# x's wide rows in four strided groups at the head of the program, y's wide rows on ScalarE's queue beside them

## The chip, the cores and the metric

The kernel runs on one core of one Trainium2 chip. The metric is device time in microseconds (us); the kernel before takes 119.74 us, the median of three runs (119.72 to 119.80). A core has engines that compute (VectorE and ScalarE here, DVE and ACT in the profile) and 16 DMA engines that move data between HBM, the chip's main memory, and SBUF, the on-chip memory of 128 partitions. SyncE (SP) computes nothing here: it issues DMAs. A DMA that is issued from SP shows in the profile as queue q1, one issued from ScalarE as q10.

## The reference

Two float32 arrays of 1024 x 4096 (16.8 MB each) are multiplied element by element, and the tanh form of GELU is applied to the product:

```
z = x * y
return (0.5 * z * (1 + np.tanh(np.sqrt(2 / np.pi) * (z + 0.044715 * z ** 3)))).astype(np.float32)
```

So 33.55 MB must be read from HBM and 16.78 MB written. Nothing is reduced or reused.

## The kernel before

The work is element by element, so the arrays are taken as flat memory. `columns` (L51) cuts each into three consecutive pieces, and each piece into 128 contiguous rows, one per partition: piece 0 has rows of 1280 elements (5 KB), piece 1 rows of 16384 (64 KB), piece 2 rows of 15104 (60,416 bytes). x stays whole in SBUF (`xs`), and the result is written over it. y has a smaller buffer (`ys`, 20,440 elements a partition): the later pieces of y go where earlier ones have been used up, so the loads of y wait for products.

The scheduling framework is closed before the first instruction (L58, L59): everything after it is in the order written, with hand-made semaphores. The order of y is piece 1, piece 2, piece 0.

- `_hoist` (L25) takes a DMA out of its place and puts it into the program's first block, ahead of the barrier with which a program opens.
- Loads before the change: x piece 0 (5 KB rows) is hoisted on SP (L79); x piece 1 (64 KB rows) is hoisted on ScalarE's queue (L80). SP then waits until x piece 0 has landed (L81), issues y piece 1 (L82) and x piece 2 (L83). It waits for the third product, issues y piece 2, waits for the fourth product, issues y piece 0 (L84 to L87).
- Compute (L91 to L109): VectorE waits for the pieces of x and y, multiplies in steps of 4096 columns (four, piece 1), 2048 and 768 (eight, piece 2) and 1280 (one, piece 0), at L98. After each product ScalarE applies GELU in place (L106).
- Stores (L111 to L115), all from SP: piece 1 once y piece 2 has landed and its GELUs are done, then piece 2, then piece 0, each when its last GELU is done. SP waits for the stores and clears the semaphores (L116 to L121).

A DMA adds 16 to its semaphore when it has landed, one for each DMA engine that carried part of it.

Of the kernel before, what the change touches and what calls it, by code (L numbers as in the profile page):

```python
# [1 line left out]

# [4 lines left out]


F32 = mybir.dt.float32
GELU = mybir.ActivationFunctionType.Gelu_apprx_tanh  # L10

PIECES = [(0, 1280), (1280, 17664), (17664, 32768)]

Y_LOADS = [(1280, 17664, 4056), (17664, 32768, 0), (0, 1280, 15104)]

Y_FREE = [0, 3, 4]

STEPS = [[4096] * 4, [2048] * 7 + [768], [1280]]  # L20
STORES = [(1280, 17664), (17664, 32768), (0, 1280)]
Y_BUF = 20440


def _hoist(nc, issued):  # L25

    here = nc.cur_bb.bb.instructions
    first = nc.main_func.blocks[0].instructions
    for ins in issued:
        del here[next(k for k, i in enumerate(here) if i is ins or i.name == ins.name)]  # L30
    engine = issued[0].engine
    at = next(
        k
        for k, i in enumerate(first)
        if i.engine == engine and type(i).__name__ == "InstDrain"
    )
    first[at:at] = issued


@with_exitstack  # L40
def kernel(
    ctx: ExitStack,
    tc: tile.TileContext,
    x: bass.AP,
    y: bass.AP,
    out: bass.AP,
):
    nc = tc.nc
    P = nc.NUM_PARTITIONS

    def columns(t, a, b):  # L51

        flat = t.flatten_outer_dims().rearrange("r c -> (r c)")
        pa, pb = next(q for q in PIECES if q[0] <= a and b <= q[1])
        return flat[P * pa : P * pb].rearrange("(p c) -> p c", p=P)[:, a - pa : b - pa]


    tc.close()  # L58
    tc.compile()  # L59

    xs = nc.alloc_sbuf_tensor("xs", [P, PIECES[-1][1]], F32).ap()
    ys = nc.alloc_sbuf_tensor("ys", [P, Y_BUF], F32).ap()
    sem_x = [nc.alloc_semaphore(f"sem_x{i}") for i in range(len(PIECES))]
    sem_y = [nc.alloc_semaphore(f"sem_y{i}") for i in range(len(Y_LOADS))]
    sem_mul = nc.alloc_semaphore("sem_mul")
    sem_act = nc.alloc_semaphore("sem_act")
    sem_o = [nc.alloc_semaphore(f"sem_o{i}") for i in range(len(STORES))]

    def load_x(i, engine=nc.sync):
        a, b = PIECES[i]  # L70
        return engine.dma_start(out=xs[:, a:b], in_=columns(x, a, b)).then_inc(sem_x[i], 16)

    def load_y(i):
        a, b, r = Y_LOADS[i]
        return nc.sync.dma_start(
            out=ys[:, r : r + b - a], in_=columns(y, a, b)
        ).then_inc(sem_y[i], 16)

    _hoist(nc, [load_x(0).ins])  # L79
    _hoist(nc, [load_x(1, nc.scalar).ins])  # L80
    nc.sync.wait_ge(sem_x[0], 16)  # L81
    load_y(0)  # L82
    load_x(2)  # L83
    for i in range(1, len(Y_LOADS)):  # L84
        if Y_FREE[i]:
            nc.sync.wait_ge(sem_mul, Y_FREE[i])
        load_y(i)  # L87

    n = 0
    done = {}  # L90
    for i, (a, b, r) in enumerate(Y_LOADS):  # L91
        for j, (xa, xb) in enumerate(PIECES):
            if xa <= a < xb:
                nc.vector.wait_ge(sem_x[j], 16)
        nc.vector.wait_ge(sem_y[i], 16)  # L95
        c = a
        for w in STEPS[i]:
            nc.vector.tensor_mul(  # L98
                out=xs[:, c : c + w],
                in0=xs[:, c : c + w],  # L100
                in1=ys[:, r + c - a : r + c - a + w],
            ).then_inc(sem_mul, 1)
            n += 1
            done[c + w] = n
            nc.scalar.wait_ge(sem_mul, n)
            nc.scalar.activation(  # L106
                out=xs[:, c : c + w], in_=xs[:, c : c + w], func=GELU
            ).then_inc(sem_act, 1)
            c += w  # L109

    for i, (a, b) in enumerate(STORES):  # L111
        if i == 0:
            nc.sync.wait_ge(sem_y[-2], 16)
        nc.sync.wait_ge(sem_act, done[b])
        nc.sync.dma_start(out=columns(out, a, b), in_=xs[:, a:b]).then_inc(sem_o[i], 16)  # L115
    for i in range(len(STORES) - 1):  # L116
        nc.sync.wait_ge(sem_o[i], 16)
    nums = sorted(s.num for s in [*sem_x, *sem_y, *sem_o[:-1], sem_mul, sem_act])
    assert nums == list(range(nums[0], nums[-1] + 1))
    nc.sync.sem_clear(range(nums[0], nums[-1] + 1))  # L120
    nc.sync.wait_ge(sem_o[-1], 16).then_inc(sem_o[-1], -16)  # L121


# [1 line left out]
_INS = ['x', 'y']  # L125
_OUTS = [((1024, 4096), 'float32')]


# [23 lines left out]
```

## Time and profile before

| what | value |
|---|---|
| median of three runs | 119.74 us |
| span of the profiled execution, first to last instruction | 118.5 us |
| execution's time beyond the span | about 1.2 us (119.74 less 118.5) |
| HBM read and written | 33.55 MB and 16.78 MB, 425 GB/s over the span |
| VectorE busy | 35.2 us (30%) |
| ScalarE busy | 31.0 us (26%) |
| x piece 0, issue to landing | 13.6 us |
| x piece 1, issue to landing | 30.4 us |
| y piece 1, issue to landing | 29.0 us |
| x piece 2, issue to landing | 46.5 us |
| y piece 2, y piece 0, issue to landing | 22.5 us, 19.7 us |
| three stores, issue to landing | 20.4, 20.9, 20.8 us |

How to read it: times in the trace start at the span's first instruction. "DMA share" is the busy share of the 16 DMA engines. In a narrow window a transfer row is counted by its start and with its whole length, so a share can be over 100% there; in wide windows this evens out. From the share of a queue, the width of the window and the number of packets the mean time of one row follows: share x 16 x width / packets. A packet is one row of one partition, or the 4-byte completion write that each DMA engine makes after its rows. There are 8 rows and one completion write of each DMA on each DMA engine (9 DMAs x 16 x 9 = 1296 packets).

### The profile page before, as it was taken

To read this page: it belongs to the slowest core of one execution; us is meant where nothing else is said; L and a number is where in the kernel's file an instruction comes from. 1 tells how busy PE (TensorE), PEld (TensorE's weight loads), DVE (VectorE), ACT (ScalarE), POOL (GpSimd) and SP (SyncE) were. 2 spreads that over 40 slices of the span, in tenths; PEclk is the share of its full clock that TensorE was granted. 3 is DMA by queue.
4 is the path that set the end of the run, shared out by engine and by line. 5 is a ranking of instruction groups with operands and counts; after the bars stand their busy time and mean duration, and the time that the engine had idled before them with its cause. 6 is when DMAs were issued, how large, how long until landed. Compare 5 with 4: busy or idle time off the path is not lost.

```text
span 118.5 us, 82 instructions
## 1 busy us (share of the span) xinstructions
DVE 35.2 (30%) x13; ACT 31.0 (26%) x14; POOL 0.2 (0%) x4
## 2 busy tenths in 40 slices
DVE  0000000000000069999920000059999940000000
ACT  4000000000000000977975000006998990000000
POOL 0000000000000000000000000000000000000000
DMA  9888899889988897797797797798899887977975
GB/s 492 382 382 382 354 575 487 354 354 398 664 354 354 354 652 326 326 652 326 326 632 347 326 632 347 326 575 354 354 531 531 354 354 326 652 326 326 652 326 221
DMA packets 1296, 50.33 MB, mean 425 GB/s; under 512 B 144, under 2 KB 144, under 8 KB 528
## 3 DMA queue, kind: packets, MB, share of 16 engines
q1 hardware_dynamic: 1152, 41.94, 82.2%
q10 hardware_dynamic: 144, 8.39, 16.5%
HBM read 33.55 MB, written 16.78 MB: 425 GB/s over the span
## 4 chain that ended last, share of the span: by engine, by line
DMA 55%; DVE 24%; ACT 3%; issue 1%; DVEq 0%
DMA ys<-in_y_dram 43%; DVE xs L98 24%; DMA xs<-in_x_dram 11%; ACT xs L106 3%; DVEq L95 0%
## 5 line engine op out<-in xcount | busy, mean ns | idle before, releaser
L98 DVE TENSOR_TENSOR xs<-xs,ys 128x2048 f32<-128x2048 f32 (+3 forms) x13 | 35.2, 2777 | 60.9 <-DMA ys<-in_y_dram 60.9
L106 ACT ACTIVATE xs<-xs 128x2048 f32<-128x2048 f32 (+3 forms) x13 | 29.7, 2301 | 65.1 <-DVE xs L98 65.1
L106 ACT ACT_TABLE_LOAD x1 | 1.3, 1283 | 1.6 <-PEq L59 1.6
L136 POOL MEMSET const-bfloat16-1.0<- 128x1 bf16 x1 | 0.1, 103 | 0.0
L136 POOL MEMSET const-uint8-127<- 128x1 uint8 x1 | 0.1, 102 | 0.0
L136 POOL MEMSET const-float32-0.0<- 128x1 f32 x1 | 0.1, 100 | 0.2 <-issue 0.2
L136 POOL MEMSET const-float32-1.0<- 128x1 f32 x1 | 0.1, 99 | 0.0
## 6 DMA issues: line engine op xcount, KB each, us to landing
xs<-in_x_dram SPq DMA_DIRECT2D x1, 7552.0 KB, 46.5
ys<-in_y_dram SPq DMA_DIRECT2D x1, 7552.0 KB, 22.5
out_dram<-xs SPq DMA_DIRECT2D x1, 7552.0 KB, 20.4
xs<-in_x_dram SPq DMA_DIRECT2D x1, 640.0 KB, 13.6
ys<-in_y_dram SPq DMA_DIRECT2D x1, 640.0 KB, 19.7
out_dram<-xs SPq DMA_DIRECT2D x1, 640.0 KB, 20.8
xs<-in_x_dram ACTq DMA_DIRECT2D x1, 30.4
ys<-in_y_dram SPq DMA_DIRECT2D x1, 29.0
```

The costliest lines, as they stand in the source:

```text
L98: nc.vector.tensor_mul(out=xs[:, c : c + w], in0=xs[:, c : c + w], in1=ys[:, r + c - a : r + c - a + w],).then_inc(sem_mul, 1)
L106: nc.scalar.activation(out=xs[:, c : c + w], in_=xs[:, c : c + w], func=GELU).then_inc(sem_act, 1)
L136: nc = _bacc.Bacc("TRN2", target_bir_lowering=False, num_devices=1)
```

## The change

x piece 1 is cut into four DMAs, each of every fourth partition (0, 4, 8, ..., then 1, 5, 9, ...), 32 rows of 64 KB each, all adding to one semaphore. The first is hoisted on SP and is the first instruction of the program. y piece 1 is hoisted on ScalarE's queue, where x piece 1 was. SP issues the other three groups, x piece 0 and x piece 2 right after the opening barrier, without waiting for anything to land. VectorE waits for 64 counts on x piece 1 instead of 16. The loads of y pieces 2 and 0, the compute and the stores stay as they were.

```diff
+GROUPS = 4
...
-    def load_x(i, engine=nc.sync):
+    def load_x(i, group=slice(None)):
         a, b = PIECES[i]
-        return engine.dma_start(out=xs[:, a:b], in_=columns(x, a, b)).then_inc(sem_x[i], 16)
+        return nc.sync.dma_start(
+            out=xs[group, a:b], in_=columns(x, a, b)[group]
+        ).then_inc(sem_x[i], 16)
 
-    def load_y(i):
+    def load_y(i, engine=nc.sync):
         a, b, r = Y_LOADS[i]
-        return nc.sync.dma_start(
+        return engine.dma_start(
             out=ys[:, r : r + b - a], in_=columns(y, a, b)
         ).then_inc(sem_y[i], 16)
 
-    _hoist(nc, [load_x(0).ins])
-    _hoist(nc, [load_x(1, nc.scalar).ins])
-    nc.sync.wait_ge(sem_x[0], 16)
-    load_y(0)
+    groups = [slice(g, None, GROUPS) for g in range(GROUPS)]
+    _hoist(nc, [load_x(1, groups[0]).ins])
+    _hoist(nc, [load_y(0, nc.scalar).ins])
+    for group in groups[1:]:
+        load_x(1, group)
+    load_x(0)
     load_x(2)
     for i in range(1, len(Y_LOADS)):
-        if Y_FREE[i]:
-            nc.sync.wait_ge(sem_mul, Y_FREE[i])
+        nc.sync.wait_ge(sem_mul, Y_FREE[i])
         load_y(i)
...
-                nc.vector.wait_ge(sem_x[j], 16)
+                nc.vector.wait_ge(sem_x[j], 16 * GROUPS if j == 1 else 16)
```

## The prediction

> **What bounds the kernel now.** I read the page first: slices, queues, chain. Then I asked the trace for stretches of time, to see where the 16 DMA engines are not moving bytes at full pace, and for the DMA queues in narrow windows, to get the time of one row.
>
> From the page:
>
> ```profile
> DVE 35.2 (30%) x13; ACT 31.0 (26%) x14; POOL 0.2 (0%) x4
> ...
> DMA packets 1296, 50.33 MB, mean 425 GB/s; under 512 B 144, under 2 KB 144, under 8 KB 528
> ...
> q1 hardware_dynamic: 1152, 41.94, 82.2%
> q10 hardware_dynamic: 144, 8.39, 16.5%
> ...
> DMA 55%; DVE 24%; ACT 3%; issue 1%; DVEq 0%
> ```
>
> The two queues together use 98.7% of the 16 engines' span, so the bound is DMA throughput. The chain names VectorE for 24% of the span, and that is misleading: while it multiplies, the queue still holds transfers. The stretches show it (length, DVE, ACT, POOL, clock, DMA share, GB/s):
>
> ```profile
> 0.00:1.00 1.00, 0.00 (x0) 0.00 (x0) 0.20 (x4) 1.00 0.00 0
> 1.00:2.30 1.30, 0.00 (x0) 0.73 (x1) 0.00 (x0) 1.00 0.93 295
> 2.30:78.20 75.90, 17.43 (x4) 15.02 (x5) 0.00 (x0) 1.00 1.00 433
> 78.20:79.10 0.90, 0.75 (x1) 0.00 (x0) 0.00 (x0) 1.00 0.90 376
> 79.10:118.10 39.00, 17.02 (x9) 15.26 (x9) 0.00 (x0) 1.00 1.00 430
> 118.10:118.50 0.40, 0.00 (x0) 0.00 (x0) 0.00 (x0) 1.00 0.00 0
> ```
>
> From 2.3 us to 118.1 us the engines are busy all the time but for a dip at 78.2 to 79.1. What a reordering of loads can win lies in three places: the first 1.0 us, in which nothing moves; the opening up to about 5 us; the dip. The chain in order of time tells which waits order the queue:
>
> ```profile
> 0.00 13.55 DMA xs<-in_x_dram
> ...
> 13.57 28.99 DMA ys<-in_y_dram
> ...
> 42.66 13.11 DVE xs L98 x3
> ...
> 55.78 22.47 DMA ys<-in_y_dram
> ```
>
> **The price of a row.** Queue lines of five narrow windows, in this order: 0 to 2.3 us (opening, 5 KB rows), 2.3 to 2.65 (first 64 KB rows), 5.0 to 5.4 (second 64 KB rows), 7.6 to 8.2 (third), 62 to 77 (60,416-byte rows):
>
> ```profile
> q1 hardware_dynamic: 75, 0.38, 52.6%
> ...
> q10 hardware_dynamic: 16, 1.05, 726.8%
> ...
> q10 hardware_dynamic: 16, 1.05, 609.8%
> ...
> q10 hardware_dynamic: 16, 1.05, 403.2%
> ...
> q1 hardware_dynamic: 102, 6.16, 94.8%
> ```
>
> Share x 16 x width / packets gives the mean row. Opening 5 KB rows: 0.526 x 16 x 2.3 / 75 = 258 ns; in 77.6 to 79.0, in full flow, the same rows take 197 ns. 64 KB rows: 2544 ns the first, 2439 the second, 2419 the third. 60,416-byte rows: 2231 ns. So each DMA engine must work 24 x 2.42 + 24 x 2.231 + 24 x 0.197 = 116.35 us, whatever the order. The span is 118.52: 1.0 before the first packet, 0.4 from the last packet to the end, and 0.75 to be found. The opening has 0.09 of idle time (0.07 of 1.3 us), 75/16 x (258 - 197) = 0.29 of slow 5 KB rows, and 0.12 + 0.02 of slow first and second 64 KB rows: 0.52. The dip is 0.09.
>
> **The spread of the 16 engines.** In the trace's record of single packets the engines take their first row between 1.01 and 1.49 us. The completion counts of x piece 0 come in from 13.01 to 13.55, those of y piece 1 from 42.01 to 42.56, those of y piece 2 from 77.71 to 78.25. So a spread of 0.54 arises in the opening and is carried unchanged. It costs at the dip: SP issues the first store only when the slowest engine has counted (78.27), its first rows start at 79.11, and the faster engines are out of work before.
>
> **The change, part by part.**
>
> *Bytes and row lengths* are the same: 0.
>
> *Completion writes.* Three more DMAs put three more 4-byte writes on each engine, 9 ns each in the packet records: +0.03 us.
>
> *Issuing.* One DMA issue takes SP 0.33 to 0.43 us. Five stand behind the barrier now (three groups, x pieces 0 and 2); the trace has SP through it at about 1.5 us, so they run to about 3.5 us. Cover: group 0 gives each engine two rows of 2.42 us, from 1.0 to 5.8 us even without y, and group 1, issued by 1.9, should flow at 3.0. SP's wait for x piece 0 (12.0 us) goes, and nothing is queued behind it that is late: 0. If the group DMAs took long to issue, the 2.8 us of margin would be used up first.
>
> *x and y piece 1 side by side.* Each engine alternates between the queues: 16 rows x 2.42 = 38.7 us, so both land at about 40.5 instead of 30.4 and 42.6. VectorE starts 2 us earlier, which is worth nothing by itself: y piece 2 is issued after the third product, 40.5 + 13.1 = 53.6, while x pieces 0 and 2 keep the queue busy until 40.2 + 8 x 0.197 + 8 x 2.231 = 59.6. Cover 6.0 us, less 0.9 from issue to flow. Alternation itself costs nothing where it is seen: from 17 to 29 us, with x and y rows of 64 KB alternating, the packet records show 2.42 us a row and no idle time. The new case differs in that both run at the same row number, so I allow 0 to 0.1.
>
> *The second half* keeps its order. y piece 2 still ends the loads but for y piece 0; VectorE needs 15.5 us from there, ScalarE the rest, and the second store is issued at 96.55 while the first one still flows until 98.7. Margin 2.1 us, unchanged: 0.
>
> *The opening*, the one term that counts. x piece 0's rows leave it and are paid at 197 ns in the middle: -0.29 at most. In their place come 64 KB rows of x, then of y. Lower bound of what these cost at a cold start: as the second rows, 0.02 for each tensor, and no idle time: 0.04, a gain of 0.48. Upper bound: the chill of 0.29 belongs to the first half microsecond of traffic whatever its shape, and x's first and y's first rows each pay 0.12 on top, with 0.09 idle and 0.02 as now: 0.64, a loss of 0.12. I take what the nearest row shows, the first 64 KB rows: 0.12 for x, 0.12 for y, 0.09 idle, 0.02 = 0.35, a gain of 0.17.
>
> *The spread.* The first DMA has 32 rows instead of 128, so the last engine should get its first row sooner. Bounds: the spread stays (0), or vanishes, and the slowest engine moves from its 78.25 to the mean of 77.97 (-0.28). I take half: -0.13.
>
> Sum: -0.17 - 0.13 + 0.03 = -0.27 us. The profiled span of 118.52 becomes 118.25, and with the same 1.2 us beside it 119.47. The bounds added up: -0.73 at one end, +0.25 at the other.
>
> [...] The row: one 128-row DMA of x piece 1 flows at 2.42 us a row on every engine, and no 32-row DMA is in this trace. [...]
>
> **The rivals.**
>
> *The opening costs the same whatever row opens it* (-0.05 to +0.25 us: 119.69 to 119.99). For it: the first 5 KB packets end between 1.44 and 1.77 us however early they start, so something warms up by the clock, not by rows. Against: ten of the sixteen first 64 KB rows pay again, at 2.3 us.
>
> *A group does not spread evenly* (slower). Every forecast above needs each group to put two rows on every engine, at full pace. If a group's 32 rows run on half of the engines, or on all but two at a time into one lane of SBUF, then x piece 1's 8 rows for an engine count double: 8 x 2.42 = +19.3 us, about 139 us. It decides as soon as one engine has three rows of a group instead of two (+2.4 us). Nothing of it shows in a trace with 128-row DMAs only; against it speaks that 4 x 32 rows stepped by four touch each run of four partitions once, as the 128-row DMA does four times. [...]
>
> *The change is hidden anyway.* If the spread and the chill stay as they are, 0.03 us of completion writes is all: 119.77.
>
> **How the numbers follow.** A cheaper opening as summed, 119.2 to 119.65: 0.56, of which 0.45 lies below 119.50. Same opening or hidden, 119.65 to 119.98: 0.23. Opening dearer by more than 0.24 us: 0.06. Uneven groups: 0.15. A measurement of this kernel can hardly tell less than 0.2%, 0.24 us, from no change. So faster 0.45; same 0.11 + 0.23 = 0.34; slower 0.06 + 0.15 = 0.21. The likeliest case's own range is 119.2 to 119.65. The range given leaves out the uneven groups and the thin ends: 119.1 to 120.0.
>
> **What would show it.** Right: first rows of 64 KB near 2.54 us, first starts closer together than 0.48 us, completion counts of y piece 2 within 0.3 us, the last of them before 78.1, x and y piece 1 landing at 40 to 41 us, a DMA share of 1.00 from 2 us on. Wrong: 64 KB rows over 2.45 us on q1 after 5 us (lanes shared), engines that idle before 40 us (uneven groups), idle engines about 3 to 8 us (late groups), a spread of 0.5 us as before. Wrong for another reason: a first packet that starts later than 1.0 us, which no row here prices.

## The result, and the profile after

The changed kernel takes 120.25 us (median of four runs, 120.16 to 120.37) against 119.73 us for the kernel before on the same chip: ratio 1.0041, 95% interval 1.0028 to 1.0054. It is slower by about half a microsecond, where the forecast was 119.47 us. The profiled execution has a span of 118.84 us and took 120.18 us.

The page of the changed kernel, with the lines that answer those of before (the bound is still DMA throughput; 48 more packets are the three additional DMAs with one completion write on each of 16 engines):

```profile
DVE 35.2 (30%) x13; ACT 31.0 (26%) x14; POOL 0.2 (0%) x4
...
DMA packets 1344, 50.33 MB, mean 424 GB/s; under 512 B 192, under 2 KB 192, under 8 KB 576
...
q1 hardware_dynamic: 1200, 41.94, 81.8%
q10 hardware_dynamic: 144, 8.39, 16.9%
...
DMA 53%; DVE 23%; ACT 3%; SPq 1%; issue 1%; DVEq 0%
```

Stretches of the changed kernel (length, DVE, ACT, POOL, clock, DMA share, GB/s):

```profile
0.00:1.00 1.00, 0.00 (x0) 0.00 (x0) 0.20 (x4) 1.00 0.00 0
1.00:4.10 3.10, 0.00 (x0) 1.28 (x1) 0.00 (x0) 1.00 1.01 338
4.10:78.50 74.40, 17.43 (x4) 14.47 (x4) 0.00 (x0) 1.00 1.00 432
78.50:79.50 1.00, 0.82 (x1) 0.00 (x0) 0.00 (x0) 1.00 1.47 615
79.50:118.40 38.90, 16.96 (x9) 15.26 (x9) 0.00 (x0) 1.00 0.98 425
118.40:118.80 0.40, 0.00 (x0) 0.00 (x0) 0.00 (x0) 1.00 0.01 0
```

From 4.1 us on nothing is worse than before: 432 GB/s up to 78.5 us, where it was 433, and from 78.5 to 118.4 us 429 GB/s, as in the 39.9 us from 78.2 to 118.1 before (a row counts where it starts, so the 615 and the 425 of the two lines belong together). In 1.0 to 4.1 us the engines count as busy (a share of 1.01), yet only 338 GB/s pass, where a share of 1.00 goes with 432 GB/s afterwards: here busy was not the same as moving at full pace. The queue lines of three narrow windows, 1.1 to 1.9 us (first rows of y piece 1), 4.1 to 4.7 (first rows of x piece 1) and 6.6 to 7.2 (second rows of y), tell what is slow:

```profile
q10 hardware_dynamic: 16, 1.05, 391.9%
...
q1 hardware_dynamic: 16, 1.05, 407.4%
...
q10 hardware_dynamic: 16, 1.05, 403.2%
```

Share x 16 x width / 16 packets: 3135 ns, 2444 ns, 2419 ns. The rows that opened the traffic lost 0.72 us on each engine. The first of them came from ScalarE's queue: SP's strided issue took 0.54 us instead of 0.38, and x's first rows found the engines already taken by y.

The chain in order of time shows that everything downstream kept its distance:

```profile
2.99 38.33 DMA xs<-in_x_dram
...
41.34 13.11 DVE xs L103 x3
...
54.47 24.12 DMA ys<-in_y_dram
```

VectorE starts 1.3 us earlier and y piece 2 is asked for 1.3 us earlier, but it lands at 78.59 instead of 78.25: the queue is full anyway (a share of 1.00 up to 78.5 us), and what was lost at the opening is still missing at the end. Bytes moved tell the same: summed over the packet records, the changed kernel is 0.15 MB behind the kernel before at 10 us, which is 0.34 us at full pace, and it is still 0.34 us behind at 110 us.

**A single number for an opening.** From the packet records I take the mean end of each engine's first wide row (64 KB), subtract that row at full pace (2.42 us) and the narrow rows done before it at their full pace (0.197 us for a 5 KB row, shorter rows in proportion). What is left is the moment from which full pace would have given the same progress; I call it the effective start, counted from the first DMA issue. Before: 5.00 - 2.42 - 0.98 = 1.60 us. After: 4.43 - 2.42 = 2.01 us. The difference, 0.41, and the completion writes, 0.03, are more than the span's growth in these two profiles (0.32, from 118.52 to 118.84); a second profile of the changed kernel had 118.98, and by its packet records 0.1 us of that was lost at the dip near 79 us.

### The profile page after: what moved, and what is told of

Same layout as the page of the kernel before. It is cut to its first block, busy times and chain, and to the rows that moved or that the text cites. A ratio compares the mean times of both kernels' runs of the same rounds, so it can differ in the third digit from the quotient of the medians.

```text
span 118.8 us, 85 instructions
## 1 busy us (share of the span) xinstructions
DVE 35.2 (30%) x13; ACT 31.0 (26%) x14; POOL 0.2 (0%) x4
## 4 chain that ended last, share of the span: by engine, by line
DMA 53%; DVE 23%; ACT 3%; SPq 1%; issue 1%; DVEq 0%
DMA xs<-in_x_dram 32%; DVE xs L103 23%; DMA ys<-in_y_dram 20%; ACT xs L111 3%; SPq L73 1%; DVEq L100 0%
## 5 line engine op out<-in xcount | busy, mean ns | idle before, releaser
L103 DVE TENSOR_TENSOR xs<-xs,ys 128x2048 f32<-128x2048 f32 (+3 forms) x13 | 35.2, 2779 | 61.3 <-DMA xs<-in_x_dram 41.3
```

Of the source, the lines that this page charges most:

```text
L103: nc.vector.tensor_mul(out=xs[:, c : c + w], in0=xs[:, c : c + w], in1=ys[:, r + c - a : r + c - a + w],).then_inc(sem_mul, 1)
```

## The experiments

**Theory A**: wide rows are slow to get going when nothing else is in flight, and x piece 0's narrow rows covered that. **Theory B**: the strided groups cost, by their longer issues. Later rivals: two queues that open together (C); a cold start that belongs to the addresses a row touches (A2) and not to time or to the first rows of any kind (A1); a fixed moment of the clock; collisions of rows a power of two apart. The batches ran on different chips, each beside the kernel before on its own chip, whose median was 119.70 to 119.91 us; ratios are to those.

### One group instead of four

```diff
-GROUPS = 4
+GROUPS = 1
```

> x piece 1 as one 128-row load at the head of SP, the rest as in the changed kernel (y piece 1 opens ScalarE's queue, x piece 0 later). Theory A (wide rows open cold: the first 64 KB rows of a program take about 3.1 us instead of 2.42, as the changed kernel's profile shows, whatever their grouping): no better than the changed kernel, 120.1 to 120.4 us, first rows of y again 2.9 to 3.4 us. Theory B (the strided groups cost: SP needs 0.47 to 0.59 us for each instead of 0.38, and x's rows come late): back to about 119.7 us, first rows near 2.5 us.

Measured: 120.13 us, 1.0018 (1.0008 to 1.0027); first rows of x, now 16 from SP, in the window 1.0 to 2.0 us:

```profile
q1 hardware_dynamic: 16, 1.05, 320.2%
```

3202 ns. The slow first rows are there without groups and on the other queue. The time left room for B, so the changed kernel was run again, first on another chip:

> The changed kernel once more, beside the next three on one chip. Theory A alone (wide rows open cold, the grouping is free): the same ratio as with one group, 1.0018, and the span of 118.8 us again. Theory A and B together: 1.003 to 1.005, so 0.2 us or more above the kernel with one group.

Measured: 120.36 us, 1.0056 (1.0042 to 1.0069). Across chips this seemed to speak for B. Then both stood on one chip:

> The changed kernel, beside the kernel with one group on the same chip. If wide rows that open idle DMA engines are the whole cause, both have the same ratio to before, within 0.1%. If the four strided issues cost too, this one is 0.1 to 0.4% above the other.

> x piece 1 in one group, beside the changed kernel on the same chip. Wide opening the whole cause: the same ratio as the changed kernel, 1.002 to 1.005. Grouping costs as well: 0.1 to 0.4% below it.

Measured: four groups 120.30 us, 1.0037 (1.0024 to 1.0050); one group 120.19 us, 1.0032 (1.0020 to 1.0044). The grouping costs 0.1 us by the medians, and the two intervals overlap; together they would still leave room for about 0.3 us. Most of the loss, by the medians, is there without it. The gap between the first two batches, 1.0018 and 1.0056, does not return on one chip.

### x piece 0 back in the opening

The changed kernel with x piece 0 at the head and all four groups behind the barrier:

```diff
-    _hoist(nc, [load_x(1, groups[0]).ins])
+    _hoist(nc, [load_x(0).ins])
     _hoist(nc, [load_y(0, nc.scalar).ins])
-    for group in groups[1:]:
+    for group in groups:
         load_x(1, group)
-    load_x(0)
```

> x piece 0 (5 KB rows) opens SP again, y piece 1 opens ScalarE's queue, x piece 1 in its four strided groups behind the barrier. Theory A: the 5 KB rows take the cold start, the first rows of y take about 2.55 us as x's did before, 119.7 to 119.8 us. Theory B: four strided groups are still issued, 120.1 to 120.3 us.

Measured: 119.91 us, 1.0001 (0.9992 to 1.0010), where the kernel before took 119.91 us on this chip. The whole loss is gone, with the strided groups, y on ScalarE's queue and the missing wait all kept. First rows of y, window 2.0 to 2.42 us:

```profile
q10 hardware_dynamic: 16, 1.05, 624.3%
```

2622 ns. At 10 us this run is 0.04 us behind the kernel before by bytes moved, where the changed kernel is 0.34. (Its profiled execution was the slowest of its twelve, 120.48 us; it lost its time later, between 45 and 80 us.) A holds, B falls.

The kernel before without its wait (`nc.sync.wait_ge(sem_x[0], 16)` taken out):

> The kernel before without SP's wait for x piece 0, so y piece 1 follows right behind the barrier and x and y piece 1 alternate from the start. Theory A: the opening is the same 5 KB rows, so 119.7 us as before (within 0.1). Rival (side-by-side streams of x and y from the start cost): 119.9 us or more. Theory B says nothing here but 119.7.

Measured: 119.94 us, 0.9998 (0.9989 to 1.0006). The 119.9 us named for the rival is reached in absolute time only because this chip ran the kernel before in 119.91 us; the ratio decides. The wait was worth nothing; streams of x and y side by side from the start cost nothing that shows within 0.1%.

### How much cover is needed

One group of x piece 1 behind the barrier, y piece 1 on ScalarE's queue ahead of it, and as the opening all, half or a quarter of x piece 0's columns (the rest later):

```diff
-    _hoist(nc, [load_x(1, groups[0]).ins])
+    _hoist(nc, [load_x(0, 0, 640).ins])      # 320, 640 or all 1280 columns
     _hoist(nc, [load_y(0, nc.scalar).ins])
...
+    load_x(1)
+    load_x(0, 640)
```

> All of x piece 0 (5 KB rows) opens SP, y piece 1 ScalarE's queue, x piece 1 whole behind the barrier. Full cover: 0.999 to 1.0005 of before, wide first rows near 2.55 us, although y opens instead of x and x and y alternate.

> Half of x piece 0 (640 columns, 2.5 KB rows) opens SP, y piece 1 ScalarE's queue, x piece 1 whole behind the barrier. If narrow rows only cover the 0.8 us that wide rows need longer to get going, half the cover (8 rows of about 0.1 us, flowing until about 2.1 us) gives back about half: 0.1 to 0.25 us over the run with all 1280 columns.

> A quarter of x piece 0 (320 columns, 1,280-byte rows, eight for each engine) opens SP, y piece 1 opens ScalarE's queue, x piece 1 whole behind the barrier. If the cold start passes with time or with the first rows of any kind (A1), y's first 64 KB rows take at most 2.7 us and the time is 0.999 to 1.0005 of before. If it belongs to the addresses that a row touches (A2), they take 3.0 us or more, as they are y's first, and the time is 1.0015 to 1.003.

Measured, with the run without cover for comparison; effective start by the packet records:

| narrow rows in the opening | ratio to before (95%) | effective start, us |
|---|---|---|
| 1280 columns, 5 KB | 1.0006 (0.9997 to 1.0014) | 1.64 |
| 640 columns, 2.5 KB | 1.0015 (1.0006 to 1.0024) | 1.65 |
| 320 columns, 1.25 KB | 1.0033 (1.0021 to 1.0046) | 1.98 |
| none (one group, same chip as the first two) | 1.0032 (1.0020 to 1.0044) | 2.00 |

With all of x piece 0, y's first rows, window 2.2 to 2.7 us:

```profile
q10 hardware_dynamic: 16, 1.05, 510.1%
```

2551 ns: the wide rows of y do as x's did before (2544), and the time, 1.0006, is level with before, if 0.0001 over the mark set. With half the cover, 0.09 us more than with all of it remains in the times, about a third of the loss and just short of the 0.1 to 0.25 us expected; the intervals of the two overlap, and the effective start of its one profile shows no loss (that execution, 120.24 us, lost its time after 10 us). So whether half the cover is enough stays open. The quarter was a miss: y's first rows took 2632 ns, under the 2.7 I had named for A1, yet the time, 1.0033, is just over the upper mark of A2. The likely reason is in the window 1.0 to 1.87 us of that run:

```profile
DMA packets 96, 0.12 MB, mean 140 GB/s; under 512 B 1, under 2 KB 96, under 8 KB 96
...
q1 hardware_dynamic: 96, 0.12, 91.3%
```

Its rows of 1,280 bytes took 0.913 x 16 x 0.87 / 95 = 134 ns, almost three times their share of a 64 KB row (2419 / 51.2 = 47): too few bytes passed while the wide rows got ready. Here the short first wide row did not tell a good opening, since the wait lay in front of it; the effective start (1.98 us) does.

### What it is not

x piece 1 alone on ScalarE's queue, nothing hoisted on SP:

```diff
-    _hoist(nc, [load_x(0).ins])
     _hoist(nc, [load_x(1, nc.scalar).ins])
-    nc.sync.wait_ge(sem_x[0], 16)
     load_y(0)
+    load_x(0)
     load_x(2)
```

> The kernel before with x piece 0 out of the opening: x piece 1 opens alone on ScalarE's queue, SP issues y piece 1, x piece 0 and x piece 2 behind the barrier. Cold by itself (theory A): first 64 KB rows 3.0 to 3.4 us although only one queue opens, 1.0015 to 1.004 of before. Rival C (two queues of wide rows that open together get in each other's way): first rows about 2.55 us, 0.998 to 1.000 of before.

Measured: 120.25 us, 1.0047 (1.0034 to 1.0059), first rows 3002 ns, effective start 1.93. It is not two queues that disturb each other; C falls.

The kernel with one group, with neither load ahead of the barrier (`_hoist` left out for both):

> The kernel with one group of x piece 1, but neither opening load is put ahead of the barrier: SP and ScalarE issue them at about 1.6 us, first rows at about 2.6 us. Everything is 1.5 us later by the issue alone. If the slow first rows belong to the clock (something that is over by about 2 us), they take 2.42 to 2.55 us here and the time is 1.009 to 1.011 of before. If they belong to being first (A, whenever it is), they take 3.0 to 3.4 us again and the time is 1.013 to 1.016.

Measured: 121.52 us, 1.0142 (1.0129 to 1.0155). Queue line of the window 2.3 to 3.1 us, where its first rows start:

```profile
q1 hardware_dynamic: 16, 1.05, 391.2%
```

3130 ns, 1.4 us later than elsewhere. It is not the clock; the effective start is again 1.89 us after the issue.

x piece 2 at the head, with rows of 60,416 bytes that do not lie a power of two apart (x piece 1 behind the barrier, so that VectorE starts late):

> x piece 2 (60,416-byte rows) opens SP and x piece 1 comes behind it; the time is of no use (VectorE starts late, y's later loads with it). Only the first rows count: if rows that lie a power of two apart collide while all engines start together, the first rows of x piece 2 take 2.23 to 2.35 us; if any wide row opens cold, 2.9 to 3.3 us.

Measured: 134.74 us in one run, and the first rows, window 1.0 to 1.8 us:

```profile
q1 hardware_dynamic: 16, 0.97, 388.8%
```

3110 ns against 2231 in flow. It is not the power of two.

Narrow rows at the addresses of the wide ones (the first 320, then the first 1280 columns of x piece 1 as the opening, the rest behind the barrier):

```diff
-    _hoist(nc, [load_x(1, groups[0]).ins])
+    _hoist(nc, [load_x(1, 0, 1280).ins])     # 320 in the first of the two runs
     _hoist(nc, [load_y(0, nc.scalar).ins])
...
+    load_x(1, 1280)
```

> The same with the first 320 columns of x piece 1: 1,280-byte rows, 64 KB apart, open SP; the rest of x piece 1 follows behind the barrier, x piece 0 later. A1: as the run with a quarter of x piece 0, 0.999 to 1.0005. If the spread of the addresses makes the cold start (A2): the narrow rows themselves take 0.5 us or more each at first and the time is 1.0015 to 1.003.

> The first 1280 columns of x piece 1 open SP: 5 KB rows as in the kernel before, but 64 KB apart, at the addresses of the wide rows; y piece 1 opens ScalarE's queue, the rest of x piece 1 and x piece 0 follow behind the barrier. If 5 KB rows help because they keep the DMA engines moving for the 1.6 us in which wide rows get nowhere, the time is 0.999 to 1.001 of before. If they help because x piece 0 lies close together in memory, 1.003 to 1.005 as with the 320 columns.

Measured: 320 columns 120.22 us, 1.0043 (1.0031 to 1.0056), effective start 1.89; 1280 columns 120.03 us, 1.0016 (1.0008 to 1.0025), effective start 1.72. The second lies between the two marks set for it. Against 1.0032 without cover, 5 KB rows give back about half of the loss in time, and most of it by the effective start, also when they lie 64 KB apart. Between them and x piece 0's rows, which lie together, 0.1% remains (1.0016 against 1.0006, on one chip but in two batches); the addresses may have that part. The 320 columns missed A2's mark in their own rows (71 ns for the first sixteen, not 0.5 us), so A2's mechanism as I stated it is not seen.

### An idle moment in the middle of the opening

The kernel before, with x piece 1's load issued behind the barrier:

```diff
-    _hoist(nc, [load_x(1, nc.scalar).ins])
+    load_x(1, nc.scalar)
```

> The kernel before, with x piece 1 issued by ScalarE behind the barrier instead of ahead of it: x piece 0 has the first 1.6 us to itself. If wide rows make no progress before about 2 us and x piece 0's 8 rows of 0.2 us cover the later issue, 0.998 to 1.000 of before, first wide rows 2.42 to 2.5 us. If ScalarE's early issue is needed (rows run out before 2.6 us), 1.001 to 1.003.

Measured: 121.14 us, 1.0112 (1.0091 to 1.0132), far over either mark. x piece 0 ran out at about 3 us (from 3.0 to 3.5 us the engines are busy for 68% by the packet records), and then the wide rows came. Window 2.9 to 4.2 us:

```profile
q10 hardware_dynamic: 16, 1.05, 230.2%
```

2993 ns. Here 8 narrow rows had gone before on every engine, and the wide rows are slow all the same. So what makes them slow is not to be first in the program; they are slow where they enter engines that have nothing else in flight. A is to be stated so. A fixed time from the issue to full pace had no run of its own. It does not sort these rows: two of them, which started 2.3 and 2.7 us after their issue, still took 3.25 and 2.92 us, while in the kernel before such rows started 2.2 to 2.5 us after theirs and took 2544 ns. The opening explains only part of this run's time: by bytes moved it is 0.70 us behind the kernel before at 10 us, and 1.19 at 110 us. The rest is lost around 60 us and mostly at the dip near 80 us, where the counts of y piece 2 came 1.08 us apart instead of 0.54.

### Consecutive partitions

```diff
-    groups = [slice(g, None, GROUPS) for g in range(GROUPS)]
+    groups = [slice(32 * g, 32 * g + 32) for g in range(GROUPS)]
```

> The changed kernel with the four groups cut as 32 consecutive partitions instead of every fourth. If rows are dealt to DMA engines and SBUF lanes by their partition, rows of x on SP's queue take longer than 2.42 us or some engines idle, and x piece 1 lands up to 19 us later: 125 to 139 us. If only the number of rows counts, as the changed kernel, 120.2 us. Theories A and B do not differ here.

Measured: 144.10 us, 1.1952 (1.1901 to 1.2004). Queue line of the window 1.0 to 2.0 us (first rows of x), and the stretches up to and after the end of x piece 1:

```profile
q1 hardware_dynamic: 16, 1.05, 489.7%
```

```profile
0.00:62.00 62.00, 0.00 (x0) 1.28 (x1) 0.20 (x4) 1.00 0.99 271
62.00:141.00 79.00, 35.21 (x13) 29.74 (x13) 0.00 (x0) 1.00 0.99 424
```

4897 ns for these first rows; the later rows of x piece 1 took 4771 ns in the mean (packet records), 1.97 times 2419, and only 271 GB/s pass until x piece 1 is in. The time is over the upper mark of 139 us. The engines are busy throughout (a share of 0.99), so the loss lies in rows that take twice as long and not in idle engines. Rows of every fourth partition took 2419 ns after the first in the changed kernel (packet records). What doubles the time of the rows of consecutive partitions is not shown.

No version beat both kernels: the best, 0.9998 to 1.0006, equal the kernel before.

## Why the prediction was wrong

- **The opening, -0.17 us: this is the step that failed.** I took the first 64 KB rows of the profile before (0.12 us over full pace) as the nearest row for wide rows that open. Those rows came at 2.3 us into engines that were busy with 5 KB rows. In idle engines the same rows took 3.0 to 3.2 us, a loss of 0.6 to 0.8. My upper bound (0.64 us of loss after the first microsecond) was too low as well: the effective start of 2.01 us is a loss of 1.01. By the same measure the kernel before lost 0.60, so the term was +0.41 (0.34 by the bytes moved at 10 us), not -0.17. The loss fell on the rows that came first, those of y (0.72 us); the first rows of x, which entered the running stream, lost 0.03 instead of the 0.12 set down for them. The bound assumed that a cold start costs the same time whatever the row's shape; the runs without cover (1.89 to 2.07 us) against those with 5 KB rows (1.59 to 1.72) refute that. The sign that I had named for another cause, a first packet later than 1.0 us, came too, at 1.13 us; with one group the first packet came at 1.01 us and the effective start was still 1.99, so it is not what was lost.
- **x piece 0's slow rows, "-0.29 at most"**: they were not waste. They moved 0.98 us worth of bytes while the wide rows got ready, and taking them out took their cover away. The working named no cover for this, since it counted them as a cost.
- **The spread, -0.13 us**: mis-sized. My 77.97 for the mean was a misreading: the landings of before give 77.93, 0.32 us ahead of the slowest. In the changed kernel the engines' first rows started 0.69 us apart (1.13 to 1.81), not closer; the counts of y piece 2 came within 0.45 us instead of 0.54, and the slowest lay 0.26 us behind the mean instead of 0.32: -0.06.
- **Completion writes, +0.03 us**: 48 more packets of 9 ns in the packet records, three on each engine, as forecast.
- **Issuing, 0**: right in effect. The issues took 0.47 to 0.59 us and SP was done at 4.7 us instead of 3.5, but group 1 came in time and the share is 1.00.
- **x and y side by side, 0**: right in effect; y landed at 36.5 and x at 41.3, not both at 40.5. In the run without the wait alternation cost nothing that shows (0.9998, interval 0.9989 to 1.0006).
- **The second half, 0**: right; 429 GB/s as before, and the first store is issued 0.02 us after y piece 2, as before.
- **The 1.2 us beside the span**: wrong. I took the median less the span of another execution. Each profiled execution since then has 1.33 to 1.35 us beside its own span, so the profiled execution of before lay about 0.1 us over the median, and my 118.25 would have made 119.6.
- **The rivals.** "The opening costs the same whatever row opens it" had the right doubt, but it was priced with the upper bounds and so ended at 119.99. "A group does not spread evenly" did not happen with every fourth partition; with consecutive ones the rows took 1.97 times as long (4771 ns against 2419), at +24 us where I had +19.3. The engines did not idle (a share of 0.99); that two rows share one lane into SBUF, the other way named for it, is not shown.
- **The split.** On one chip four strided parts took 120.30 us and one load 120.19, ratios of 1.0037 and 1.0032 with overlapping intervals: the parts brought nothing over one load, and they were not the main reason for the loss.

## What to carry to other kernels

Where the profile shows the DMA engines busy all the time, as here (a share of 1.00 from 4.1 to 78.5 us), look at the stretch in which they start. In these kernels a short load with 5 KB rows, issued ahead of the wide ones, moved bytes while the wide rows got going; it was worth 0.2 to 0.6% (ratios from 1.0018 to 1.0056 without it), and rows of 1,280 bytes were too little (1.0033). It has to last until the wide rows go: where it ran out before they came, they took 2993 ns again. Price a load at the head of a program, or after a gap, by rows that entered idle engines (2993 to 3202 ns for 64 KB here), not by the first rows of a tensor that entered a running stream (2544 ns). The one load that was split here was better stepped over its partitions (1.0037 of before, 2419 ns a row) than cut into blocks of 32 (1.1952, 4771 ns a row).

## What the runs showed of the hardware

- 64 KB and 59 KB rows that read HBM and enter idle DMA engines took 3.0 to 3.2 us for the first row (3135, 3202, 3002, 3130, 3110, 2993 ns in six kernels), against 2.23 to 2.42 in flow. 64 KB rows that came behind 5 KB rows took 2.49 to 2.62 us (2544, 2622, 2551, 2491 ns in four kernels). The first stores, which write to HBM, took 2.45 us in the packet records of before, but their engines had stood idle for only 0.09 us in the mean (the dip, 10% of 0.9 us), so they are no clean comparison. Why these loads need the longer start is not shown.
- 5 KB rows lost less at the start: an effective start of 1.59 to 1.66 us after the issue when x piece 0 opens whole, against 1.89 to 2.07 when wide rows open.
- At the head of the program, a DMA of 32 rows of every fourth partition held SP for 0.54 us, one of 128 rows 0.38 and one of 32 consecutive partitions 0.39; so the stepped DMA was the slower to issue, and here it let the other queue's rows go first. Behind other issues the lengths say less: x piece 0, with 128 rows, took 0.59 us behind the groups and 0.38 at the head.
- 32 consecutive partitions halved the pace of x piece 1's load (4771 ns a row after the first), every fourth partition did not (2419).
